# One attention chain over both token halves, two query tiles, two state tiles, and the recurrence's second half begun one attention step sooner

## The chip, the cores and the metric

The kernel runs on one core of a Trainium2 chip. A core has five engines that run side by side, each working through its own instructions strictly in the order in which they stand: TensorE (PE, matrix products; its weight loads are shown apart as PEld), VectorE (DVE), ScalarE (ACT), GpSimd (POOL) and SyncE (SP), which here issues nearly all DMAs. An instruction that waits for a semaphore holds up everything behind it on its engine; a DMA that waits on SP holds up the DMAs behind it.

The metric is the device time of the whole program in microseconds (us), lower is better, as the median of several runs. Of one execution there is also a profile; the times of instructions below come from that one.

## What is computed

One layer of a streaming encoder: a token mixer (sliding-window attention with sinks in one half of the channels, a gated linear recurrence in the other), a cross-attention into 256 memory tokens, and a SwiGLU feed-forward block, each between two RMSNorms. The change touches the token mixer alone. Its two halves, shortened:

```python
def swa_with_sinks(q, k, v, sinks):     # 8 query heads, 2 key heads, head size 64
    # a frame in chunk c (64 frames) reads every frame of chunks c-2 .. c
    s = einsum('bnqhgd,bnkhd->bhgqk', qc, kband) * 64 ** -0.5
    p = softmax(concat([s, sink]))[..., :L]
    return einsum(p, vband)

def hgrn2(q, f_logit, i, g, lb, onorm_g):    # 4 heads of 128
    # S_t = diag(f_t) S_{t-1} + k_t i_t^T,  o_t = S_t^T q_t, in chunks of 64
    ...
    return rms_norm(o, onorm_g) * silu(g)

u = rms_norm(x, g_mix_pre)
z = u @ w_in                        # 1024 -> 2816: q, k, v, and the recurrence's q, f, i, g
y = concat([ya, yh]) @ w_out
```

All tensors are float32; the token count is 2048 and the model width 1024. Products are made of three products of a high and a low part (a matmul on each pair but low times low).

## The kernel before

The 2048 tokens make 16 pairs of chunks of 128 tokens (NT = 16), and two halves of 1024 (NPB = 8 pairs each). `run` calls `mix`, which records the whole layer; a scheduler of the language then puts each engine's instructions in an order of its own, with dependencies kept, so that the order of recording is a priority and not the order on the chip.

`mix` goes through these stages:

- `in_first` makes the first half's input projection z and two blocks of 128 columns of the second half's. z goes to DRAM (`z_d`).
- The stage that the change touches runs three generators side by side, each cut into steps by `yield`: `swa` (attention, one pair of chunks a step), `hgrn` (recurrence, one pair a step) and `in_proj` (the second half's remaining 20 column blocks of the projection, 128 columns a step, long runs of matmuls of 128x512 in lines 156 to 158 that fill PE between the others' pieces). Before: first `swa` and `hgrn` over pairs 0 to 7 (lines 218 to 226), then a second `swa` over pairs 8 to 15 (lines 227 to 234) with the next column blocks and, in `side`, the sums of the output projection's weight blocks (`sums`, `combined`), which load `w_out` and store `out_s`.
- In the `xp` pool (lines 238 to 246) `fold_cross` folds the cross-attention's weights (32 steps), while `hgrn` runs over pairs 8 to 15 and `phases` prepares the output projection's tiles (splits written to `T`, loads `z<-in_w_out_dram`).
- After that `phases` makes the output projection, the cross-attention and the feed-forward block. That is the longest part, and the change does not touch it.

`swa` is a pipeline of two stages: at each step `swa_front` of one pair is recorded, then `swa_back` of the pair before. `swa_front` loads the queries of four heads (`qd`, lines 758 to 761), splits them on ACT (line 763) and DVE (line 764) into `qs`, does that again for the other four heads, loads the keys (`kr`, high part on POOL, low part on DVE, line 983 within `split2`), transposes the values (line 779), and makes scores (lines 798, 799), masked minimum (803) and exponential (807). `swa_back` transposes the probabilities (832), splits them (`pth` on ACT 836, `ptl` on DVE 837), multiplies by the values (841, 842) and stores. One call of `swa` takes one step more than it has pairs; the last step has only a back.

The tile `qd` has one buffer. The two query loads of a pair, and those of the next pair, therefore use the same memory one after the other. `qs` has two buffers.

`hgrn` is a pipeline of three stages: `hgrn_state` of pair n-1, `hgrn_front` of pair n, `hgrn_last` of n-2, `hgrn_out` of n-1. `hgrn_state` scales the state W of the pair before on POOL (line 907) and adds the new product on DVE (line 908) into a new tile W; `hgrn_out` multiplies the queries by the state that was there before (line 919). W has three buffers, each as large as a `qd` tile (512 floats a partition).

PSUM has eight banks here, of four kinds with two buffers each: g (the projection's), t, s and h. A generator is given the kinds that it may use: `swa` s and t in the first half, s, t and h in the second; `hgrn` h in the first, g and t in the second.

Of the kernel before, what the change touches and what calls it, by code (L numbers as in the profile page):

```python
# [11 lines left out]
F32 = mybir.dt.float32  # L12
# [6 lines left out]
P = 128  # L19
# [9 lines left out]
NPB = TB // P  # L29
NT = T // P  # L30
# [6 lines left out]
def f32(ap):  # L37
    return ap.bitcast(F32)
# [10 lines left out]
class Layer:  # L49
# [144 lines left out]
    def mix(self):  # L194
        tc, I = self.tc, self.I
        kw = dict(reuse_waits="tile")
        with contextlib.ExitStack() as left:
            def pool(name, at, **k):
                return at.enter_context(tc.tile_pool(name=name, bufs=1, **k, **kw))

            self.mc = pool("mc", left)
            self.r_x = self.cst.tile([P, NT], F32, name="r_x")
            with (
                tc.tile_pool(name="t1", bufs=3, **kw) as self.ts,
                tc.tile_pool(name="t2", bufs=3, **kw) as self.tb,
                tc.tile_pool(name="s1", bufs=2, side="right", **kw) as self.st_pool,
                contextlib.ExitStack() as at,
            ):
                self.banks(at, "ps1", **MOST)
                self.raws = 3  # L210
                u = self.in_first()
            self.banks(left, "ps2", **FOUR)
            self.hg = pool("hg", left)
            self.wp = pool("wp", left)
            self.io = pool("io", left)
            with tc.tile_pool(name="sw", bufs=1, side="right", **kw) as self.sw:
                self.zero_tiles()
                swa = self.swa(range(NPB), "st")
                hgrn = self.hgrn(range(NPB), "h")
                cols = self.in_proj(1, u)  # L220
                next(cols)
                for _ in swa:
                    next(hgrn)
                    next(cols)
                for _ in hgrn:
                    pass
                swa = self.swa(range(NPB, NT), "sth")
                self.out_sums, side = self.sums("out_s", self.w_out, 4, lambda: self.io_tile("u"), lambda: self.io_tile("x"))
                side = side()
                next(side)  # L230
                for _ in swa:
                    next(cols)
                    for _ in range(4):
                        next(side, None)
                for _ in cols:
                    pass
            phases = self.phases(self.jobs(), None, lambda: self.io_tile("z"))
            with tc.tile_pool(name="xp", bufs=1, side="right", **kw) as self.xp:
                fold = self.fold_cross()
                for i, _ in enumerate(self.hgrn(range(NPB, NT), "gt")):  # L240
                    for _ in range(2):
                        next(fold)
                    if 2 <= i < 10:
                        next(phases)
                for _ in fold:
                    pass
            left.close()
            with (
                tc.tile_pool(name="t3", bufs=3, **kw) as self.ts,
                tc.tile_pool(name="t4", bufs=3, **kw) as self.tb,  # L250
                tc.tile_pool(name="s3", bufs=2, side="right", **kw) as self.st_pool,
                contextlib.ExitStack() as at,
            ):
                self.banks(at, "ps3", **MOST)
                self.raws = 4
                for _ in phases:
                    pass
# [132 lines left out]
    def zero_tiles(self):  # L390
        nc, ph = self.nc, self.hg

        self.wmask = self.sw.tile([P, M], F32, name="wmask")
        nc.vector.memset(self.wmask, 0.0)
        nc.vector.memset(self.wmask[0:64, 192:256], BIG)
        nc.vector.memset(self.wmask[64:128, 0:64], BIG)

        cm = self.io.tile([P, P], F32, tag="u", name="cm", bufs=2)
        nc.vector.memset(cm, 1.0)
        nc.gpsimd.affine_select(cm, cm, [[1, P]], ALU.is_ge, 0.0, base=0, channel_multiplier=-1)  # L400
        nc.vector.memset(cm[0:64, 64:128], 0.0)
        self.cmask = ph.tile([P, P], I32, name="cmask")
        nc.vector.tensor_copy(self.cmask, cm)

        self.atz = []
        for i in range(2):
            a = ph.tile([P, 4, P], F32, name=f"atz{i}")
            nc.gpsimd.memset(a, 0.0)
            self.atz.append(a)
        self.vst_prev = None  # L410
        self.W = ph.tile([P, 4, P], F32, tag="W", name="W0", bufs=3)
        nc.gpsimd.memset(self.W, 0.0)

    ORDER = [(4, 5), (0, 1), (2, 3)] + [(10 + h, 6 + h) for h in range(4)] + [(c, c + 1) for c in range(14, 22, 2)]
# [334 lines left out]
    def swa_front(self, n, kinds):  # L749
        nc, ph = self.nc, self.sw  # L750
# [3 lines left out]
        kinds = itertools.cycle(kinds)  # L754

        qs = []
        for g in range(2):
            qd = ph.tile([P, 4, P], F32, tag="qd", name=f"qd{n}_{g}")
            qsrc = z[g * 256:(g + 1) * 256, t0:t0 + P].rearrange("(h d) t -> d h t", d=64)
            self.load(qd[0:64], qsrc)  # L760
            self.load(qd[64:128], qsrc)
            q = ph.tile([P, 4, P], F32R, tag="qs", name=f"qs{n}_{g}", bufs=2)
            nc.scalar.activation(q, qd, AF.Copy, scale=-0.125)
            nc.vector.scalar_tensor_tensor(q[64:128], qd[64:128], -0.125, f32(q[64:128]), ALU.mult, ALU.subtract)
            qs.append(q)
# [23 lines left out]
        for g in range(2):  # L789
            mn = self.small("w_mn", 4)  # L790
            den = self.small("w_den", 4)
            for i2 in range(2):
# [7 lines left out]
                for r in range(2):  # L800
                    i = 2 * i2 + r
# [98 lines left out]
    def hgrn_state(self, n, kinds, kt, vt):  # L900
        nc, ph = self.nc, self.hg
        prev = self.W
        W = self.W = ph.tile([P, 4, P], F32, tag="W", name=f"W{n}", bufs=3)
        ps = self.bank(kinds[0])
        for h in range(4):
            nc.tensor.matmul(ps[:, h * P:(h + 1) * P], kt[:, h, :], vt[:, h, :], start=True, stop=True)
        nc.gpsimd.tensor_tensor(W, prev, self.G[:, n, :, 1].unsqueeze(2).broadcast_to([P, 4, P]), ALU.mult)
        nc.vector.tensor_tensor(W, ps.rearrange("p (h t) -> p h t", h=4), W, ALU.add)
        return prev

    def hgrn_out(self, n, kinds, q6, at, vt, W):
        nc, ph = self.nc, self.hg
        sg = ph.tile([P, 4, P], F32, tag="sg", name=f"sg{n}")
        self.load(sg, self.z_d[C_GH:C_GH + 512, n * P:(n + 1) * P].rearrange("(h p) t -> p h t", p=P))
        ps = self.bank(kinds[-1])
        for h in range(4):
            hs = slice(h * P, (h + 1) * P)
            nc.tensor.matmul(ps[:, hs], at[:, h, :], vt[:, h, :], start=True, stop=False)
            nc.tensor.matmul(ps[:, hs], q6[:, h, :], W[:, h, :], start=False, stop=True)
        ss = self.small("h_ss", 4)  # L920
        on = ph.tile([P, 4, P], F32, tag="on", name=f"on{n}")
        for h in range(4):
            nc.scalar.activation(on[:, h, :], ps[:, h * P:(h + 1) * P], AF.Square, accum_out=ss[:, h:h + 1])
        vv = self.small("h_vv", 4)
        nc.gpsimd.tensor_scalar(vv, ss, 1.0 / P, EPS, ALU.mult, ALU.add)
        rs = self.small("h_rs", 4)
        nc.gpsimd.tensor_tensor(rs, vv, self.mhalf[:, 0:4], ALU.pow)
        nc.vector.tensor_tensor(on, ps.rearrange("p (h t) -> p h t", h=4),
                                rs.unsqueeze(2).broadcast_to([P, 4, P]), ALU.mult)
        return on, sg  # L930
# [28 lines left out]
    def swa(self, pairs, kinds):  # L959
        last = None  # L960
        for n in itertools.chain(pairs, (None,)):
            cur = None if n is None else (n, kinds) + self.swa_front(n, kinds)
            if last is not None:
                self.swa_back(*last)
            last = cur
            yield
# [783 lines left out]
```

## Time and profile before

| | |
|---|---|
| median of 3 runs | 2604.39 us (2603.98 to 2605.17) |
| profiled execution, its own time | 2610.75 us |
| its span, first to last instruction | 2609.0 us |
| mean granted TensorE clock | 0.996 |
| DMA moved | 506.03 MB, mean 194 GB/s |
| first attention instruction on `qs` to the last | 280.4 to 607.6 us |
| recurrence's last state update | 741.9 us |

The profiled execution is 6.36 us longer than the median of the runs shown; sums over its rows are differences, which are then taken off the median.

How to read what follows: a row of the page or of a view names the engine, the source line, what is written and read, the form and the count. "Idle before" is time in which that engine did nothing, with what ended it. In a table by stretches of time, the first column is the stretch in us from the span's start, then its length and, for each engine, busy time and number of instructions; then the granted TensorE clock (1.00 is full speed), the busy share of the DMA engines and GB/s.

### The profile page before, as it was taken

Reading aid. Unit: us, or ns where it says so; the run is one execution under the profiler, and the core shown is the slowest. Engines: PE = TensorE matmul, PEld = TensorE weight load, DVE = VectorE, ACT = ScalarE, POOL = GpSimd, SP = SyncE. Lnnn points to the kernel's source line nnn. Section 1 sums busy time; section 2 is a strip of 40 time slices with the busy share of each in tenths; the row PEclk is TensorE's granted clock in tenths of the full one; section 3 lists DMA queues with packets and bytes.
Section 4 is the critical chain, followed back from the end, with each engine's and each line's share of the span. In section 5 each row is a group of like instructions: output and inputs, shape, how many; then the busy total and the mean of one; then the engine's idle time right before and its main releaser. Section 6 shows DMA issues by size and latency. Waiting matters only on the chain.

```text
span 2609.0 us, 34953 instructions
## 1 busy us (share of the span) xinstructions
PE 2555.2 (98%) x12371; PEld 2138.3 (82%) x12371; DVE 1752.0 (67%) x2759; ACT 1259.7 (48%) x2633; POOL 435.2 (17%) x612
## 2 busy tenths in 40 slices
PE   9999999999999999999999999999999999999998
PEld 8878788787898887888878888888888888888886
DVE  7785488877555778778885655566666556564656
ACT  5553366555555556565563333344333334453543
POOL 4231334231311323222310000000000000000022
PEclk9999999999999999999999999999999999999999
DMA  5445655675887986765974622353566434576888
GB/s 186 145 162 177 172 160 157 192 228 157 239 269 268 308 288 231 222 233 186 317 248 131 202 93 75 105 194 121 177 200 196 154 130 159 191 210 177 264 215 219
DMA packets 363663, 506.03 MB, mean 194 GB/s; under 512 B 20960, under 2 KB 249312, under 8 KB 363488
## 3 DMA queue, kind: packets, MB, share of 16 engines
q1 hardware_dynamic: 357440, 481.77, 57.0%
q0 software_dynamic: 6048, 22.02, 4.7%
q8 instruction: 97, 1.59, 0.2%
q14 instruction: 78, 0.64, 0.1%
HBM read 337.00 MB, written 166.72 MB: 193 GB/s over the span
## 4 chain that ended last, share of the span: by engine, by line
PE 79%; DMA 9%; DVE 5%; ACT 3%; issue 2%; POOL 1%; SPq 0%; DVEq 0%; POOLq 0%; ACTq 0%
PE psm L1117 22%; PE psm L1119 22%; PE psm L1118 22%; PE psg L158 1%; PE psg L157 1%; PE psg L156 1%; PE pss L1369 1%; DMA qd<-z_d 1%; DMA z<-in_w_out_dram 1%; DMA row<-y_d 1%; ACT T L980 1%; DMA raw<-in_wo_x_dram 1%; DMA u_d<-row 1%; DVE T L983 0%; DMA row<-d_s 0%
## 5 line engine op out<-in xcount | busy, mean ns | idle before, releaser
L1117 PE MATMUL psm<-T,S 128*128 128x512 f32 x2695 | 1043.8, 391 | 12.1 <-ACT part L1132 9.3
L1118 PE MATMUL psm<-T,S 128*128 128x512 f32 x2695 | 1049.0, 390 | 2.1 <-DVE T L983 2.0
L1119 PE MATMUL psm<-T,S 128*128 128x512 f32 x2695 | 1038.5, 390 | 3.9 <-DVE S L983 3.9
L1117 PEld LDWEIGHTS psm<-T,S 128*128 128x128 f32 x2695 | 506.2, 188 | 121.7 <-ACT part L1132 9.6
L1119 PEld LDWEIGHTS psm<-T,S 128*128 128x128 f32 x2695 | 506.3, 188 | 110.7 <-DVE S L983 5.6
L1118 PEld LDWEIGHTS psm<-T,S 128*128 128x128 f32 x2695 | 506.3, 188 | 106.9 <-DVE T L983 3.7
L983 DVE TENSOR_TENSOR S<-sraw,S 128x512 fp32r<-128x512 f32 (+1 forms) x319 | 217.2, 688 | 215.4 <-ACT S L980 199.3
L980 ACT ACTIVATE S<-sum 128x512 fp32r<-128x512 f32 (+1 forms) x314 | 188.7, 619 | 358.1 <-PE psm L1119 269.3
L983 DVE TENSOR_TENSOR S<-sum,S 128x512 fp32r<-128x512 f32 (+1 forms) x372 | 249.7, 681 | 49.0 <-ACT S L980 32.9
L1132 ACT ACTIVATE part<-psm 128x512 f32<-128x512 f32 x273 | 161.7, 597 | 242.8 <-PE psm L1119 220.9
L980 ACT ACTIVATE S<-sraw 128x512 fp32r<-128x512 f32 (+1 forms) x272 | 167.4, 616 | 112.3 <-PE psm L1119 99.5
L1495 POOL DMA_DIRECT2D row<-y_d x28 | 25.8, 923 | 1112.7 <-DVE row L1681 1020.2
L983 DVE TENSOR_TENSOR T<-row,T 128x1024 fp32r<-128x1024 f32 (+1 forms) x120 | 141.5, 1194 | 58.2 <-ACT T L980 57.6
L156 PE MATMUL psg<-u,whi 128*128 128x512 f32 x320 | 129.5, 405 | 0.0
L1466 ACT ACTIVATE junk<-row 128x512 f32<-128x512 f32 x160 | 99.7, 624 | 60.9 <-DVE row L1488 29.5
L157 PE MATMUL psg<-u,whi 128*128 128x512 f32 x320 | 128.0, 400 | 0.0
L158 PE MATMUL psg<-u,wlo 128*128 128x512 f32 x320 | 127.9, 400 | 0.0
L980 ACT ACTIVATE T<-row 128x1024 fp32r<-128x1024 f32 x120 | 120.0, 1027 | 12.6 <-DMA row<-in_w_down_dram 5.2
L982 POOL TENSOR_SCALAR S<-sum 128x512 fp32r<-128x512 f32 x58 | 54.2, 935 | 292.9 <-PE psm L1119 231.4
L1632 DVE TENSOR_TENSOR row<-psm,part 128x512 f32<-128x512 f32 x66 | 43.7, 687 | 61.9 <-PE psm L1119 61.8
L1641 DVE TENSOR_TENSOR part<-psm,part 128x512 f32<-128x512 f32 x60 | 39.8, 688 | 62.4 <-PE psm L1119 62.2
L1092 DVE TENSOR_TENSOR sum<-sraw,sraw 128x512 f32<-128x512 f32 (+1 forms) x93 | 63.8, 686 | 18.9 <-DMA sraw<-in_w_in_dram 5.7
(362 smaller groups left out, 3695.6 us busy)
## 6 DMA issues: line engine op xcount, KB each, us to landing
sraw<-in_w_gate_dram SPq DMA_DIRECT2D x44, 512.0 KB, 3.9
sraw<-in_w_up_dram SPq DMA_DIRECT2D x44, 512.0 KB, 3.9
hid_d<-row SPq DMA_DIRECT2D x44, 512.0 KB, 2.7
h_d<-row SPq DMA_DIRECT2D x32, 512.0 KB, 5.1
y_d<-row SPq DMA_DIRECT2D x32, 512.0 KB, 3.5
sraw<-hid_d SPq DMA_DIRECT2D x32, 512.0 KB, 5.2
row<-y_d POOLq DMA_DIRECT2D x28, 512.0 KB, 7.3
sraw<-in_w_in_dram SPq DMA_DIRECT2D x44, 256.0 KB, 3.8
```

Source lines behind the costliest of these rows:

```text
L156: nc.tensor.matmul(ps, ah, bh, start=(i == 0), stop=False)
L157: nc.tensor.matmul(ps, ah, bl, start=False, stop=False)
L158: nc.tensor.matmul(ps, al, bh, start=False, stop=(i == n - 1))
L980: self.nc.scalar.activation(hi, raw, AF.Copy)
L982: self.nc.gpsimd.tensor_scalar(hi, raw, 1.0, 1.0, ALU.mult, ALU.mult)
L983: self.nc.vector.tensor_tensor(lo, raw, f32(hi), ALU.subtract)
L1092: nc.vector.tensor_tensor(t, a, b, op)
L1117: nc.tensor.matmul(ps, s[:, 0, k, :], t[:, 0, k, :], start=st, stop=False, **kw)
L1118: nc.tensor.matmul(ps, s[:, 0, k, :], t[:, 1, k, :], start=False, stop=False, **kw)
L1119: nc.tensor.matmul(ps, s[:, 1, k, :], t[:, 0, k, :], start=False, stop=sp, **kw)
L1132: nc.scalar.activation(t, ps, AF.Copy)
L1466: self.nc.scalar.activation(junk, a, AF.Square, scale=float(D) ** -0.5, accum_out=to)
```

## The change

The diff, whole but for its comments' place:

```diff
-                swa = self.swa(range(NPB), "st")
+                swa = self.swa(range(NT), lambda n: "st" if n < NPB else "sth")
                 hgrn = self.hgrn(range(NPB), "h")
                 cols = self.in_proj(1, u)
                 next(cols)
-                for _ in swa:
+                for _ in range(NPB + 1):
+                    next(swa)
                     next(hgrn)
                     next(cols)
                 for _ in hgrn:
                     pass
-                swa = self.swa(range(NPB, NT), "sth")
                 self.out_sums, side = self.sums("out_s", self.w_out, 4, ...)
                 side = side()
                 next(side)
-                for _ in swa:
+                pairs = self.hgrn(range(NPB, NT), "gt")
+                for i, _ in enumerate(swa, NPB + 2):
                     next(cols)
+                    if i == NT + 1 - 0:
+                        next(pairs)
                     for _ in range(4):
                         next(side, None)
                 for _ in cols:
                     pass
...
                 fold = self.fold_cross()
-                for i, _ in enumerate(self.hgrn(range(NPB, NT), "gt")):
+                for _ in range(2):
+                    next(fold)
+                for i, _ in enumerate(pairs, 1):
                     for _ in range(2):
                         next(fold)
                     if 2 <= i < 10:
                         next(phases)
...
-        self.W = ph.tile([P, 4, P], F32, tag="W", name="W0", bufs=3)
+        self.W = ph.tile([P, 4, P], F32, tag="W", name="W0", bufs=2)
...
-            qd = ph.tile([P, 4, P], F32, tag="qd", name=f"qd{n}_{g}")
+            qd = ph.tile([P, 4, P], F32, tag="qd", name=f"qd{n}_{g}", bufs=2)
...
-        W = self.W = ph.tile([P, 4, P], F32, tag="W", name=f"W{n}", bufs=3)
+        W = self.W = ph.tile([P, 4, P], F32, tag="W", name=f"W{n}", bufs=2)
...
     def swa(self, pairs, kinds):
         last = None
         for n in itertools.chain(pairs, (None,)):
-            cur = None if n is None else (n, kinds) + self.swa_front(n, kinds)
+            cur = None if n is None else (n, kinds(n)) + self.swa_front(n, kinds(n))
```

So there is one `swa` over all 16 pairs with 17 steps in place of two calls with 9 each: the front of pair 8 is recorded in the step with the back of pair 7, before the last step of the first recurrence and before the loads of `w_out`. The second half's loop has 8 steps and takes 8 column blocks and 32 pieces of `side` in place of 9 and 36; two column blocks in place of one remain after it. In its last step (i is 17, with the back of pair 15) the first step of the second recurrence is recorded, which is the front of pair 8. The first two steps of `fold_cross` come before the recurrence goes on; each later recurrence step stands beside the same fold steps as before, one recurrence step ahead. `qd` gets a second buffer and W loses its third.

## The prediction, made before the changed kernel was run

> **What bounds the kernel now.** I read the page first (busy time by engine, the chain that ended last), then the table by stretches over the part that the change touches, then what PE waited for there.
>
> ```profile
> span 2609.0 us, 34953 instructions
> PE 2555.2 (98%) x12371; PEld 2138.3 (82%) x12371; DVE 1752.0 (67%) x2759; ACT 1259.7 (48%) x2633; POOL 435.2 (17%) x612
> ...
> PE 79%; DMA 9%; DVE 5%; ACT 3%; issue 2%; POOL 1%; SPq 0%; DVEq 0%; POOLq 0%; ACTq 0%
> ```
>
> PE is the bound: 98% busy, 79% of the chain. The change adds and removes no matmul, so it can only shift PE's idle time, 2609.0 - 2555.2 = 53.8 us in all, and the time at half clock. The part that it touches is 283 to 790 us:
>
> ```profile
> core 0: us, PE busy (x) PEld busy (x) DVE busy (x) ACT busy (x) POOL busy (x), PEclk, DMA share, GB/s
> 283.00:310.00 27.00, 22.44 (x107) 19.04 (x108) 15.31 (x52) 10.93 (x42) 5.74 (x11) 0.87 0.69 182
> 310.00:500.00 190.00, 188.17 (x1102) 162.04 (x1101) 155.34 (x364) 120.11 (x351) 72.73 (x109) 1.00 0.53 157
> 500.00:520.00 20.00, 16.94 (x73) 13.04 (x72) 18.72 (x41) 11.29 (x33) 6.18 (x9) 0.91 0.99 260
> 520.00:640.00 120.00, 118.35 (x616) 99.11 (x615) 94.21 (x240) 66.79 (x185) 27.63 (x44) 1.00 0.60 186
> 640.00:660.00 20.00, 14.72 (x102) 12.62 (x102) 12.73 (x21) 12.52 (x29) 6.15 (x8) 1.00 0.96 271
> 660.00:690.00 30.00, 28.03 (x219) 27.35 (x219) 19.93 (x27) 14.72 (x31) 9.30 (x8) 0.94 0.85 237
> 690.00:790.00 100.00, 96.19 (x751) 91.80 (x750) 47.17 (x69) 52.32 (x129) 21.43 (x30) 1.00 0.81 262
> ```
>
> The steady stretches are full: 1.8 us idle in 310 to 500, 1.7 in 520 to 640. The idle time sits at four joints: the first attention steps (4.6 us), the change of halves at 500 (3.1), the change from attention to the fold at 640 (5.3) and the stretch after it (2.0). At three of them the granted clock also falls, which costs PE the stretch times what is missing from 1.00: 27 x 0.13 = 3.5 us, 20 x 0.09 = 1.8, 30 x 0.06 = 1.8. That makes joints of 8.1, 4.9, 5.3 and 3.8 us, 22.1 us in all. PE's waits in this part (us in total, times, longest) say what ended them:
>
> ```profile
> PE pst L798 <- DVE qs L764: 3.2, 1, 3.2
> PE psh L841 <- ACT pth L836: 3.0, 2, 2.8
> PE psg L890 <- ACT atz L881: 1.7, 1, 1.7
> PE pst L895 <- DMA v<-z_d: 1.5, 1, 1.5
> PE pss L798 <- DVE qs L764: 1.4, 1, 1.4
> ...
> PE pst L799 <- DVE kl L983: 0.9, 2, 0.6
> PE pst L879 <- ACT T L980: 0.8, 1, 0.8
> ...
> PE psg L906 <- ACT kt L892: 0.6, 1, 0.6
> ```
>
> **The change, part by part.** *Two query tiles.* With one tile, each query load waits until ACT and DVE have taken the one before. The chain of waits through the second pair's front shows it (start, length, what):
>
> ```profile
> 290.19 5.65 DMA qd<-z_d
> 295.95 0.64 ACT qs L763
> 296.61 1.11 DVE qs L764
> 297.74 0.58 SPq L75
> 298.37 3.13 DMA qd<-z_d
> 301.61 0.64 ACT qs L763
> 302.27 0.70 DVE qs L764
> 303.02 0.58 PE pst L798
> ```
>
> The second load is issued at 297.74, when DVE is done with the first, and PE waits for it until 303.02. With two tiles both loads leave together: in the changed program's order the second query load stands directly behind the first on SP, ahead of the keys, in this pair and the one before. The landing, SP's 0.58 and the second ACT and DVE pieces (3.13 + 0.64 + 0.70) then overlap the first's, and the 3.2 us wait with the clock loss behind it goes. What is new: the loads of keys and values stand behind two more query loads, and on DVE the second query piece stands ahead of the low key part, which PE waits for:
>
> ```profile
> L764 DVE SCALAR_TENSOR_TENSOR qs<-qd,qs x32: 689/690/1103, 281.1 to 607.6; 64x512 fp32r<-64x512 f32 x32
> ...
> DMA to landing us min/median/max: 2.7/3.5/8.2
> ```
>
> So of the 8.1 us I leave the key wait of 0.6 and one more DVE piece of 0.7, and take 8.1 - 1.3 = 6.8. Bounds: 8.1 if the keys land as before; 2.3 if the idle time only halves and the clock loss of 3.5 stays. The single wait of 1.4 (the fifth row of the waits) is the same tile at another pair: take 1.4, bounds 0 and 1.4.
>
> Here the Trainium skill ("TensorE: Matmul & The Clock Gate", section on the HAM clock gate) says that PE falls to half clock after a whole idle window of about 3.4 us. The rows above show the clock fall after single waits of 3.2 and 2.8, so the trace disagrees; by the rule none of these gaps would cost clock, and the first joint's term would be 6.8 - 3.5 = 3.3 us, an estimate.
>
> *One chain over both halves.* No drain and refill at pair 8. The joint at 500 is, though, a query wait too: ACT stood for a query load, and the probabilities' split that PE wanted (L836) stood behind it and its followers on ACT:
>
> ```profile
> 500.77 1.24 SPq L75 DMA_DIRECT2D qd<-z_d  x2
> ...
> 509.46 0.63 ACT L763 ACTIVATE qs<-qd 128x512 fp32r<-128x512 f32 x1 [4.06 <-DMA qd<-z_d]
> ...
> 512.05 0.57 ACT L836 ACTIVATE pth<-pss 128x512 fp32r<-128x512 f32 x1
> ```
>
> The load took 8 us, since it came behind a burst of `w_out` loads (DMA share 0.99). The second tile and a step of lead let it be issued before the burst: in the changed order pair 10's loads stand ahead of the larger part of it. But the burst stays, and another load may now be the late one (pair 9's keys stand behind two `w_out` loads). I take 3.0 of 4.9; bounds 0 and 4.9.
>
> *The recurrence one step sooner.* At 640 PE meets pair 8's front with nothing to cover it: waits of 1.7 (atz), 0.6 (kt) and 0.8 (pair 10's scores behind a `T` split on ACT). In the changed order pair 8's scores and value transposes stand among the matmuls of the last column block, and its key copy further ahead still, so those are covered: 3.1 us. The 1.5 for `v`, whose one buffer is free only after pair 8's transposes, I leave. Moved along are pair 8's four loads, which pass the remaining attention loads on SP, and 0.25 MB each (128 x 4 x 128 floats) is little beside the half megabyte of a column block's weights (128 x 8 x 128). Bounds 0 (the wait for `v` takes up what the others leave) and 5.3.
>
> In the stretch after it, ACT waited for a `w_out` load with the fold's weight split behind it:
>
> ```profile
> 672.74 1.06 ACT L980 ACTIVATE T<-z 128x1024 fp32r<-128x1024 f32 x1 [6.53 <-DMA z<-in_w_out_dram]
> 673.71 1.04 ACT L980 ACTIVATE whi<-raw 128x1024 fp32r<-128x1024 f32 x1
> ```
>
> In the changed order this weight split and the next stand ahead of that `T` split, so PE has two more column blocks to work on before the DMA matters. I take 2.0 of 3.8; bounds 0 and 3.8.
>
> *Two state tiles.* The scaling of the state (POOL) now overwrites the tile that the output of the pair before still reads (L919), so it must wait for those matmuls; behind it on POOL stand the query scaling, the norm's small pieces, key splits and the weight splits of the projection.
>
> ```profile
> L907 POOL TENSOR_TENSOR W<-W,G x16: 1042/1044/2022, 261.7 to 731.9; 128x512 f32<-128x512 f32 x16
> ...
> L908 DVE TENSOR_TENSOR W<-psg,W x8: 680/682/693, 649.2 to 741.9; 128x512 f32<-128x512 f32 x8
> ...
> 726.91 0.39 PE L919 MATMUL pst<-W,q 128*128 128x128 f32 x2
> ...
> 729.17 0.69 DVE L908 TENSOR_TENSOR W<-psg,W 128x512 f32<-128x512 f32 x1 [3.98 <-PE psg L906]
> ```
>
> One of the tighter places: output read at 726.91, next state add at 729.17, so 2.3 us of room for a scaling of 1.04. That fits, with PE working on the fold meanwhile. If it stops fitting, each pair costs at most 1.04 + 0.68 = 1.7 us, 15 pairs 25.9. I take 1.0; bounds 0 and 25.9.
>
> *Another order everywhere in the stage.* The scheduler reorders some thousand PE rows. The next row that could move is the 1.8 us of the long steady stretch (a gain at best); at worst there is another joint like that at 500, 4.9 us. I take a loss of 2.5.
>
> **Sum.** 6.8 + 1.4 + 3.0 + 3.1 + 2.0 - 1.0 - 2.5 = 12.8 us. The profiled execution took 2610.75 us by its own clock (span 2609.0 and 1.75 around it), so the like of it would be 2598.0. It lies 6.36 above the median of the runs, and 2604.4 - 12.8 = 2591.6 us.
>
> **The rivals.**
> 1. *The joints from 500 on are bound by DMA, not by the order.* For it: DMA shares of 0.99, 0.96, 0.85 there, and a query load that took 8 us. Against it: the shares fall to 0.60 between, so work can be shifted, and the waits named are ACT's order. Then only the two query terms remain: 6.8 + 1.4 - 1.0 - 2.5 = 4.7, 2599.7 us.
> 2. *The change does not do what it says.* The waits that leave are replaced by waits for keys or values that land as late, since attention loads were late by the burst and by landing times of 2.7 to 8.2 us, whatever their buffer. Against it: the 5.7 us from one query landing of the pair to the other (290.19 + 5.65 to 298.37 + 3.13) are plain. 2604 us, give or take 3.
> 3. *Slower: the two state tiles.* POOL waits for PE's output matmuls at each pair, and PE then waits for the splits behind. For it: POOL runs in order, and the room is only 2.3 us late in the fold. Against it: the page has POOL busy for 17% of the span, and the table by stretches for 73 of the 190 us of the long steady one. Full price: 13.8 of gains without W, less 25.9, is 12.1 us slower, 2616.5 us. It decides from 13.8 / 15 = 0.9 us a pair on.
>
> **How the numbers follow.** Chances: forecast 0.62, first rival 0.17, second 0.09, third 0.12. A measurement of this kernel can tell about 0.2%, 5.2 us, from no change. Faster than 2599.2: 0.61 of the forecast and 0.08 of the first rival, 0.69. Within: 0.01, 0.09 and 0.06, 0.16. Slower than 2609.6: 0.12 and 0.03, 0.15. All upper bounds together (23.5 us) give 2580.9, which is unlikely; the range of 2583 to 2607 leaves some 0.05 below and 0.14 above, and the forecast's own range is 2584 to 2599.
>
> **What would show it.** Right: in the first attention steps no PE wait of over 1.5 us for `qs` and a clock of 1.00 after 300 us; query loads issued in pairs of two halves each; ACT's waits for `qd` well below before; pair 8's front inside the last column block; no PE wait for atz at the fold's start. Wrong: POOL waiting at L907 (L912 in the changed file) for PE with kh or whi late behind it; PE waits for kh or kl that grow by what the query waits lose; a new half-clock stretch in 430 to 640. Everything from 790 us on should be as before but earlier; a difference there would mean that something I did not price has moved.

## The result, and the profile after

The changed kernel took 2592.02 us (median of 6 runs, 2587.06 to 2595.59) against 2604.65 for the kernel before: a ratio of 0.9948, 95% interval 0.9937 to 0.9960, 12.6 us faster. The forecast was 2591.6.

The page of the changed kernel's profiled execution (2587.36 us), the lines that answer to those of before:

```profile
span 2585.7 us, 34998 instructions
...
PE 2548.3 (99%) x12371; PEld 2135.9 (83%) x12371; DVE 1747.9 (68%) x2759; ACT 1261.0 (49%) x2633; POOL 428.4 (17%) x612
...
PE 83%; DMA 7%; DVE 4%; ACT 3%; issue 2%; POOL 1%; SPq 0%; DVEq 0%; POOLq 0%; ACTq 0%
```

PE's idle time in the span fell from 53.8 to 37.4 us (2585.7 - 2548.3), and its busy time, for the same matmuls, by 6.9 us, in part because PE ran less at half clock (mean granted clock 0.998, before 0.996). The same stretches as before:

```profile
283.00:310.00 27.00, 27.00 (x151) 23.22 (x150) 19.01 (x66) 15.63 (x54) 6.26 (x14) 1.00 0.76 216
310.00:500.00 190.00, 189.43 (x1104) 163.94 (x1103) 159.78 (x367) 124.40 (x361) 75.21 (x115) 1.00 0.58 176
500.00:520.00 20.00, 19.57 (x102) 16.18 (x102) 19.70 (x52) 10.77 (x31) 5.34 (x7) 1.00 1.08 324
...
640.00:660.00 20.00, 20.00 (x168) 19.83 (x168) 14.30 (x18) 11.85 (x26) 3.80 (x6) 1.00 0.94 254
660.00:690.00 30.00, 28.80 (x243) 28.57 (x242) 13.96 (x24) 14.53 (x41) 12.79 (x16) 1.00 0.76 248
```

The first steps lose nothing now (before: 4.6 us idle and clock 0.87). The change from attention to the fold has moved forward, to 620 to 640 us, as all in front of it takes less time:

```profile
620.00:640.00 20.00, 16.62 (x105) 14.95 (x104) 10.94 (x16) 11.44 (x25) 3.20 (x5) 0.91 0.89 246
```

Here 3.4 us are idle and 20 x 0.09 = 1.8 lost to the clock. That is one of the prediction's signs of being wrong, a new half-clock stretch in 430 to 640 us; in the second execution of the changed kernel (below) this stretch lost 3.2 us and no clock. PE's longest waits from 270 to 790 us, in all, times and longest:

```profile
PE pst L900 <- DMA v<-z_d: 1.7, 1, 1.7
PE pst L900 <- ACT whi L126: 1.2, 1, 1.2
PE psg L895 <- issue: 1.2, 1, 1.2
PE psh L158 <- DVE wlo L988: 1.0, 1, 1.0
```

No wait for `qs` is left, and the first row is the wait for `v` that the prediction left in place. What the two new tile counts did shows in the views of the tiles. First what the instructions on `qd` waited for, and the landing times (the first row is that of before):

```profile
  DMA qd<-z_d: 56.7, 18
...
  ACT qs L768: 9.4, 5
  DMA qd<-z_d: 3.7, 2
...
DMA to landing us min/median/max: 2.7/3.3/6.2
```

ACT stood for query loads 56.7 us in 18 waits before, and 3.7 us in two now. Then the view of line 912, the scaling of the state on POOL (907 before), with what it waited for, and who waited for it:

```profile
L912 POOL TENSOR_TENSOR W<-W,G x16: 1042/1046/2005, 259.4 to 716.6; 128x512 f32<-128x512 f32 x16
...
  PE pst L924: 25.7, 4
  PE psh L924: 10.1, 3
...
who waited for it (us, times):
  DVE W L913: 1.7, 1
```

POOL does stand for the output's matmuls, 35.8 us in seven waits, but only one state addition waits for the scaling itself, 1.7 us, and no wait of PE in this part names POOL.

The two first profiles differ by 23.4 us, the medians by 12.6: the first execution of before was a long one, that of the changed kernel a short one. So every term below is read from medians, and from the profiles only where, and by what wait.

### The profile page after: what moved, and what is told of

It reads as the page before. It is cut to its first block, busy times and chain, and to the rows that moved or that the text cites. A ratio compares the mean times of both kernels' runs of the same rounds, so it can differ in the third digit from the quotient of the medians.

```text
span 2585.7 us, 34998 instructions
## 1 busy us (share of the span) xinstructions
PE 2548.3 (99%) x12371; PEld 2135.9 (83%) x12371; DVE 1747.9 (68%) x2759; ACT 1261.0 (49%) x2633; POOL 428.4 (17%) x612
## 4 chain that ended last, share of the span: by engine, by line
PE 83%; DMA 7%; DVE 4%; ACT 3%; issue 2%; POOL 1%; SPq 0%; DVEq 0%; POOLq 0%; ACTq 0%
PE psm L1122 23%; PE psm L1124 23%; PE psm L1123 22%; PE psg L156 2%; PE psg L157 2%; PE psg L158 2%; PE pss L1374 1%; DMA row<-y_d 1%; DMA raw<-in_wo_x_dram 1%; DMA u_d<-row 1%; DMA h1t_d<-row 1%; DMA row<-h_d 1%; ACT junk L1471 1%; ACT T L985 0%; PE pss L837 0%
## 5 line engine op out<-in xcount | busy, mean ns | idle before, releaser
L812 ACT ACTIVATE S<-S,w_mn 128x256 f32<-128x256 f32 (+1 forms) x128 | 63.1, 495 | 28.6 <-DVE w_mn L808 28.3
```

Source lines behind the costliest of these rows:

```text
L812: nc.scalar.activation(s[:, r, o:], s[:, r, o:], AF.Exp, bias=mn[:, i:i + 1], scale=-1.0, accum_out=den[:, i:i + 1])
```

## The experiments

All runs, with the kernel before run on the same chip beside them:

| kernel | query tiles | state tiles | one chain | early recurrence | median us (range) | before | ratio (95%) |
|---|---|---|---|---|---|---|---|
| before, again | 1 | 3 | no | no | 2603.8 (2601.1 to 2611.7) | 2604.7 | 1.0002 (0.9991 to 1.0012) |
| changed, again | 2 | 2 | yes | yes | 2591.9 (2588.0 to 2596.1) | 2604.7 | 0.9955 (0.9942 to 0.9968) |
| state tiles alone | 1 | 2 | no | no | 2604.3 (2598.2 to 2609.1) | 2604.7 | 0.9997 (0.9988 to 1.0006) |
| query tiles | 2 | 2 | no | no | 2609.8 (2604.8 to 2615.9) | 2604.7 | 1.0021 (1.0011 to 1.0032) |
| chain alone | 1 | 3 | yes | no | 2610.3 (2606.8 to 2612.8) | 2604.9 | 1.0016 (1.0005 to 1.0026) |
| chain, state tiles | 1 | 2 | yes | no | 2602.6 (2598.5 to 2609.6) | 2604.0 | 0.9988 (0.9978 to 0.9998) |
| early alone | 1 | 3 | no | yes | 2604.1 (2600.0 to 2608.9) | 2604.9 | 0.9999 (0.9990 to 1.0008) |
| changed, one query tile | 1 | 2 | yes | yes | 2598.8 (2597.3 to 2612.5) | 2604.9 | 0.9983 (0.9972 to 0.9994) |
| changed, late recurrence | 2 | 2 | yes | no | 2598.0 (2595.8 to 2603.2) | 2604.9 | 0.9975 (0.9965 to 0.9984) |
| changed, two calls | 2 | 2 | no | yes | 2603.4 (2598.6 to 2607.2) | 2604.1 | 0.9996 (0.9987 to 1.0004) |
| query tiles, blocks held | 2 | 2 | no | no | 2600.1 (2596.4 to 2609.8) | 2604.1 | 0.9984 (0.9973 to 0.9995) |
| changed, still sooner | 2 | 2 | yes | sooner | 2592.7 (2586.3 to 2599.6) | 2604.1 | 0.9955 (0.9941 to 0.9969) |

**Both kernels again.** No edit.

> The kernel before, unchanged: a second profiled execution of it, since the first one (2610.75 us) lay 6 us above the median of the runs (2604.4). If the idle time of the four joints belongs to the program, PE again has some 15 us idle in 283 to 690 us and three stretches at half clock, at the first attention steps, near 513 and near 677 us. If the half-clock stretches are a matter of the single execution, the shorter execution (2602 to 2606) lacks one or two of them, 2 to 4 us each, and the median gain of the change is smaller than the difference of the two first profiles (23.4 us) for that reason.

> The changed kernel, unchanged: a second profiled execution, since the first one (2587.36 us) was the shortest but one of six (median 2592.0). Expected 2592 us, plus or minus 2. If the joints' gain belongs to the program, the first attention steps again run without a wait for qs and at clock 1.00, and what the longer executions have more lies elsewhere. If the gain at the first steps is luck, a half-clock stretch shows there again, 3.4 us.

The second execution of before (2606.71 us), three of its stretches:

```profile
283.00:310.00 27.00, 22.88 (x119) 19.68 (x118) 15.56 (x51) 10.93 (x42) 5.67 (x12) 0.94 0.66 183
...
500.00:520.00 20.00, 19.55 (x102) 16.18 (x101) 17.22 (x40) 10.38 (x28) 4.71 (x7) 1.00 0.98 264
...
640.00:660.00 20.00, 16.27 (x112) 15.03 (x113) 12.17 (x18) 11.23 (x27) 10.06 (x11) 0.91 1.01 282
```

The first steps and the joint at 640 belong to the program: 4.1 and 3.7 us idle with a half-clock stretch each. The joint at 500 does not. It lost 4.9 us in the first execution and 0.45 in this one. The changed kernel's second execution has the first stretch full and at clock 1.00 again. At 500 it is now the changed kernel that loses, 2.2 us, after 0.4 in its first execution:

```profile
500.00:520.00 20.00, 17.78 (x90) 14.24 (x89) 17.29 (x46) 9.08 (x28) 6.09 (x7) 1.00 1.08 287
```

**Two query tiles, two state tiles; two state tiles alone.** In the kernel before:

```diff
-        ... tag="W", name="W0", bufs=3)
+        ... tag="W", name="W0", bufs=2)
-        ... tag="W", name=f"W{n}", bufs=3)
+        ... tag="W", name=f"W{n}", bufs=2)
```

and, for the run with two query tiles, also

```diff
-            qd = ph.tile([P, 4, P], F32, tag="qd", name=f"qd{n}_{g}")
+            qd = ph.tile([P, 4, P], F32, tag="qd", name=f"qd{n}_{g}", bufs=2)
```

> The kernel before with two query tiles and, to make room for the second, two state tiles; two attention calls and the recurrence's start as before. By my sum: 6.8 us at the first steps and 1.4 at the single wait, less 1.0 for the state tiles, so about 7 us faster, 2597 (2594 to 2601). If the two later edits carry the change and keys land as late as queries did, less than 3 us faster, 2602 or more. If the query tile carries everything, 12 us faster, 2592.

> The kernel before with two state tiles in place of three and nothing else. By my sum 1 us slower, 2605.5 (2604 to 2607). By the rival that POOL's wait for the output matmuls stops the splits behind it, up to 1.7 us a pair, 10 to 25 us slower, 2614 or more. If the scaling is hidden everywhere, no difference.

The state tiles cost nothing. The query tiles, in place of gaining 7 us, lost 5. The run with two query tiles, stretches of its profile:

```profile
283.00:310.00 27.00, 27.00 (x149) 23.06 (x148) 19.04 (x68) 15.37 (x53) 6.11 (x13) 1.00 0.78 220
...
620.00:640.00 20.00, 14.99 (x71) 10.44 (x70) 17.36 (x40) 13.14 (x31) 1.59 (x5) 0.91 0.52 160
640.00:660.00 20.00, 13.86 (x75) 12.60 (x76) 12.14 (x17) 13.07 (x29) 6.02 (x7) 0.74 0.98 253
```

The first steps gain as forecast, and it is given back at the next joint: from 620 to 640, 5.0 us idle and 1.8 of clock, from 640 to 660, 6.1 and 5.2. PE's timeline there shows the waits (in brackets), and the row below it is ACT's:

```profile
621.20 0.39 PE L158 MATMUL psg<-u,wlo 128*128 128x512 f32 x1
...
629.39 0.50 PE L841 MATMUL psh<-pth,vst 128*128 128x512 f32 x1 [2.24 <-ACT pth L836]
...
643.26 2.07 PE L906 MATMUL psg<-vt,kt 128*128 128x128 f32 x8 [4.83 <-ACT vt L897]
```

```profile
641.51 1.06 ACT L980 ACTIVATE T<-z 128x1024 fp32r<-128x1024 f32 x1 [6.27 <-DMA z<-in_w_out_dram]
```

The longest of these waits is not attention's: PE stands 4.8 us for the recurrence's `vt`, which ACT makes, and ACT had stood 6.3 us for a load of `w_out`. Attention's part lies before it. The projection's last matmul is at 621.2. All the matmuls of attention's last steps that stand behind it have nothing to cover their waits for ACT and DVE, as PE's groups from 621.3 to 640 us show (shapes, count, busy, mean, idle before):

```profile
L842 PE MATMUL psh<-ptl,vst 128*128 128x512 f32 x8 | 4.4, 555 | 0.0
L841 PE MATMUL psh<-pth,vst 128*128 128x512 f32 x8 | 4.0, 494 | 3.2 <-ACT pth L836 3.2
L832 PE MATMUL pss<-ident,S 128*128 128x128 f32 x12 | 3.4, 334 | 0.0
L832 PE MATMUL pst<-ident,S 128*128 128x128 f32 x12 | 3.3, 327 | 0.2 <-DVE w_mn L803 0.2
```

That is 24 transposes and 16 products. In the first profile of before they are no transpose and 4 products, in the changed kernel none: there the last product starts at 623.89 and the projection's last matmul at 624.79. The projection gets ahead of attention with two query tiles, and it was the cover (that is, the work that keeps PE busy while attention's pieces wait).

**One chain alone; early recurrence alone.**

```diff
-                swa = self.swa(range(NPB), "st")
+                swa = self.swa(range(NT), lambda n: "st" if n < NPB else "sth")
...
-                for _ in swa:
+                for _ in range(NPB + 1):
+                    next(swa)
                     next(hgrn)
                     next(cols)
...
-                swa = self.swa(range(NPB, NT), "sth")
```

> The kernel before with one attention chain over both halves, and nothing else: one query tile, three state tiles, the recurrence's second half begun in the fold as before. By my sum 3.0 us faster, 2601.7 (2599 to 2605): the joint near 500 us mends, the first steps and the joint near 640 stay. New theory, from the run with two query tiles: what decides at 640 is how much of attention's tail (lines 832, 841, 842) is left when the projection's matmuls end; there it was 24 transposes and 16 products, with two state tiles alone 8 and 12. The chain starts attention's second half a step sooner, so by it no such matmul is left behind the projection's end and the joint near 640 mends as well: 5 to 8 us faster, 2597 to 2600.

```diff
-                for _ in swa:
+                pairs = self.hgrn(range(NPB, NT), "gt")
+                for i, _ in enumerate(swa, NPB + 1):
                     next(cols)
+                    if i == NT + 1:
+                        next(pairs)
...
-                for i, _ in enumerate(self.hgrn(range(NPB, NT), "gt")):
+                for _ in range(2):
+                    next(fold)
+                for i, _ in enumerate(pairs, 1):
```

> The kernel before with the recurrence's second half begun in the last step of the second attention call, and nothing else. By my sum 3.1 at 640 us and 2.0 behind it, 5 us faster, 2599.6 (2597 to 2603). By the new theory attention's tail sets that joint, and pair 8's front ahead of it pushes the tail further behind the projection's end: less than 2 us faster, or slower, 2603 to 2608.

Neither gains. The chain alone is 5 us slower, though no product of attention stands behind the projection's end in it; so the tail is not all there is. Two places in its profile, PE's timeline and ACT's waits from 520 to 600 us:

```profile
549.81 0.79 PE L842 MATMUL psh<-ptl,vst 128*128 128x512 f32 x1 [2.89 <-DVE ptl L837]
...
645.09 1.62 PE L879 MATMUL pst<-qq,k 128*128 128x192 f32 x4 [5.28 <-DMA k<-z_d]
```

```profile
ACT qs L763 <- DMA qd<-z_d: 13.3, 4, 6.6
```

With one query tile a query load fell into the burst of `w_out` loads (DMA share 1.07 from 540 to 550 us, landing up to 11.5 us in this run), ACT stood for it 6.6 us, and PE went on at half clock behind the 2.9. (DVE, whose `ptl` PE waited for, had itself stood 4.1 us for the DMA `out_s<-u` until 545.88, so the query load is one of two late DMAs there.) At 640 the next pair's scores wait 5.3 us for keys of the recurrence. The early recurrence alone moved a wait: pair 8's front is covered, and PE stands for the next pair's query load:

```profile
652.83 0.89 PE L884 MATMUL pst<-qq,k 128*128 128x192 f32 x4 [3.16 <-DMA qq<-z_d]
```

**The chain with two state tiles.** As the chain alone, with W's two edits from above.

> One attention chain with one query tile, as in the run that was 5 us slower, but with two state tiles as in the changed kernel, so that the three edits can be set against each other with the state tiles alike. If the chain with one query tile is slower because a query load falls into the burst of w_out loads (there PE lost 2.9 us and its clock near 550 us) and because pair 8's loads are late at 640, it is slower again, 2607 to 2612, with ACT waiting for qd by 5 us or more in 520 to 600. If that loss was a chance of one order of the scheduler, which other state tiles shift, it is as before or faster, 2600 to 2605.

2602.6 us, 7.7 less than with three state tiles (6.8 less when each is taken from the runs of before beside it). In its profile ACT's waits for `qd` from 520 to 600 us are

```profile
ACT qs L763 <- DMA qd<-z_d: 3.6, 4, 1.5
```

So the second expectation came true: the loss of the chain alone was of one order, which other tile counts shift. How the scheduler comes to that order was not followed.

**The changed kernel, one part undone at a time.** One query tile (`bufs=2` taken away from `qd`):

> The changed kernel with one query tile, all else as changed (one chain, two state tiles, early recurrence). By my sum it loses 8.2 us against the changed kernel: 2600 (2597 to 2602), with the wait for qs and the half-clock stretch back at the first attention steps. By the rival that the order carries the change and the second query tile brings nothing in the end, as it brought nothing alone: 2592 to 2595.

The recurrence begun in the fold as before:

```diff
-                pairs = self.hgrn(range(NPB, NT), "gt")
-                for i, _ in enumerate(swa, NPB + 2):
+                for _ in swa:
                     next(cols)
-                    if i == NT + 1 - 0:
-                        next(pairs)
...
-                for _ in range(2):
-                    next(fold)
-                for i, _ in enumerate(pairs, 1):
+                for i, _ in enumerate(self.hgrn(range(NPB, NT), "gt")):
```

> The changed kernel with the recurrence's second half begun in the fold as before, all else as changed (one chain, two query tiles, two state tiles). By my sum it loses 5 us against the changed kernel: 2597 (2595 to 2600). By the new theory the chain has put attention's tail under the projection already, and pair 8's front alone is left uncovered at 640: 3 to 5 us lost, and no matmul of attention behind the projection's end. If the early start is what mends the joint that two query tiles spoiled, it loses 10 us or more, 2602 or higher.

Two attention calls (the two query and state tiles of the earlier run, with the early recurrence's edit):

> The changed kernel without the single chain: two attention calls, two query tiles, two state tiles, the recurrence's second half begun in the second call's last step. In PE's order 24 transposes and 16 products of attention stand behind the projection's end, as with two query tiles alone. By the theory of the tail the chain is what takes them away, and this kernel is not faster than before: 2604 to 2610. By my sum it loses only the 3.0 us of the chain against the changed kernel: 2595.

Against the changed kernel's 2591.9 the three lose 6.9, 6.1 and 11.5 us. With one query tile the wait is back, in the first steps' stretch and in PE's waits:

```profile
283.00:310.00 27.00, 23.55 (x121) 19.97 (x120) 17.16 (x62) 12.92 (x47) 6.12 (x12) 0.94 0.59 165
```

```profile
PE pst L803 <- DVE qs L769: 2.7, 1, 2.7
```

That is 3.5 us idle and 1.6 of clock, 5.1 of the 6.9. With the late recurrence the two waits of pair 8's front are back that were named for before:

```profile
PE psg L890 <- ACT atz L881: 2.1, 1, 2.1
PE psg L906 <- ACT kt L892: 1.3, 1, 1.3
```

With two calls attention's tail lies behind the projection again, and the joint costs 4.9 us idle and 3.8 of clock:

```profile
620.00:640.00 20.00, 15.10 (x72) 12.15 (x71) 14.37 (x26) 11.86 (x22) 0.20 (x1) 0.81 0.66 195
```

The changed kernel lost 3.4 and 1.8 in that stretch (above), so 3.5 of the 11.5 us are seen here. From 620 to 690 us, idle time and clock together, this kernel loses 10.8 us, and the changed kernel 6.4 and 5.5 in its two executions. In attention's tail there PE waits 2.9 us for `ptl`, 2.1 of it at once. The execution that was profiled is the shortest of 11, 4.9 us under their median.

**Query tiles, column blocks held back.** As the run with two query tiles, and

```diff
-                for _ in swa:
-                    next(cols)
+                for i, _ in enumerate(swa):
+                    if i > 2:
+                        next(cols)
```

> Two query tiles and two state tiles in the kernel before, as in the run that was 5 us slower, but the second attention call's first three steps take no column block of the projection, so that four are left at its end. In the order of PE's instructions 8 transposes and 12 products of attention then stand behind the projection's end, as with two state tiles alone, in place of 24 and 16. By the theory of attention's tail the joint near 640 us costs about what it costs with two state tiles alone, and the gain at the first steps stays: 2598 to 2601. If the two query tiles lose elsewhere, or the tail is not what costs, it stays at 2607 to 2611.

2600.1, within the expected 2598 to 2601: with 20 matmuls of attention behind the projection in place of 40 the kernel is 9.7 us faster. Its one profile (2609.79 us) is of the longest of 12 executions, but the joint can be read in it:

```profile
620.00:640.00 20.00, 16.06 (x91) 12.89 (x89) 15.22 (x31) 13.33 (x28) 1.01 (x3) 1.00 0.63 190
640.00:660.00 20.00, 17.05 (x110) 16.02 (x109) 14.49 (x20) 12.79 (x29) 6.79 (x9) 0.83 1.13 264
```

That is 6.9 us idle and 3.4 of clock, 10.3 in all, where the run without the hold lost 18.1 and two state tiles alone, also with 20 behind, 10.6. So the joint gave back 7.8 of the 9.7 us. It does not part the tail from the late load: ACT's longest wait for a load of `w_out` in 625 to 700 us fell with it, from 6.3 to 2.6 us.

**The recurrence sooner still.** `if i == NT:` in place of `NT + 1 - 0`.

> The changed kernel with the recurrence's second half begun one attention step sooner still, with the back of pair 14. What is left at the joint is PE's wait for v (1.7 us) and a half-clock stretch near 633 us. If the loads of pair 8 are what is late there, an earlier start takes 2 to 4 us more: 2588 to 2590. If it collides with attention's own tail, or v's one buffer decides, no gain or a loss: 2592 to 2597.

2592.7: no gain. In its profile the 1.7 us wait for `v` is gone from PE's list, and in its place

```profile
PE pst L900 <- DVE on L933: 3.4, 1, 3.4
PE psg L884 <- ACT mT L126: 1.8, 1, 1.8
PE pst L923 <- ACT vt L902: 1.6, 1, 1.6
```

## Why the prediction was right, and where it was not

The time came out at 0.4 us from the forecast, in a sum with two wrong terms.

*Two query tiles* (6.8 + 1.4 = 8.2): right in company, with the wait and the place that were named; undoing them in the changed kernel costs 6.9 us. The 8.1 us from which the term was taken were one execution's: the second lost 4.1 idle and 1.6 of clock there. The clock did not fall after the wait of 3.2 us, as the prediction reads it, but in its midst, at 301.51 us.

*The recurrence one step sooner* (3.1 + 2.0 = 5.1): right in size, 6.1 when undone, but only the 3.1 shows where it was placed, in the waits for `atz` and `kt` (2.1 + 1.3). The 2.0 for the stretch from 660 to 690 us does not: with the late recurrence that stretch lost 0.3 us, and in the changed kernel's two executions 1.2 and 1.8. That the size fits is in part luck. The wait for `v` stayed, as said.

*Two state tiles* (1.0): 0.4 us faster by the medians, and the interval holds no loss over 0.06%, 1.6 us. The third rival, slower through POOL, is out: POOL waits, and of PE's waits only one of 0.3 us, in the second execution, is for the state's addition behind it.

*One chain over both halves* (3.0): mis-sized. Undone it costs 11.5 us. The term was read from a joint at 500 us that lost 4.9 us in one execution and 0.45 in the next, and with the change 0.4 and 2.2, so no run shows that the chain mends it. What the chain is seen to bring beside two query tiles lies elsewhere: it keeps attention's last steps among the projection's matmuls. The prediction's part on the chain spoke of "no drain and refill at pair 8", never of where the last pair's drain falls.

*Another order everywhere* (2.5 loss, at worst 4.9): the step that failed. The orders of single edits cost more than their gains. From the kernel with two state tiles on (2604.3), two query tiles cost 5.5 us where the sum had a gain of 8.2, some 14 us off; the chain's time changes by 7.7 with the number of state tiles. The edits' effects do not add: alone they come to 5.5 (query tiles), -1.7 (chain) and, taken from its own run beside before, -0.8 (early recurrence), 3 us slower in sum (each known to some 3 us), while together they are 12.4 faster. Undone one at a time they are worth 6.9 + 11.5 + 6.1 = 24.5, twice the whole. The sum of 12.8 lay between these by luck as much as by reading: a chain term that was too small stood for an interaction that it did not know.

The first rival (the joints from 500 us on are bound by DMA, 4.7 us gained) is out for the whole, since undoing the chain or the early start loses 11.5 or 6.1 us; in single edits it was right: there PE or ACT stood for a late load next (`qq` 3.2, `k` 5.3, `z` 6.3 on ACT). The second (keys take the place of queries) is out: of waits for attention's keys PE has none in the changed kernel's first execution and 0.2 us in the second.

That the joint at 640 is a matter of the tail's cover rests on the run with held blocks, which hit its expected time and lost 7.8 us less at the joint, and on the two runs with 40 matmuls behind it, each slower than its counterpart with fewer (2609.8 against 2600.1, 2603.4 against 2591.9). It is not the whole rule: two state tiles alone leave 20 behind and lose nothing in time, the chain alone leaves none and is slower, and a `w_out` load that comes late at the joint is a rival that no run parts from it. Of the chain's 11.5 us some 5 are seen at the joint; where the rest comes from stays open: executions of one kernel differ by some 10 us, and one profile of each does not resolve 8 us spread over 300.

## What to carry to other kernels

Where a scheduler orders the engines, price an edit by the order that it makes, in the built program, and not by the wait that it removes: count which matmuls still stand behind the end of the work that covers them, as a first question and not as a rule. Test a change of several parts by undoing one part at a time as well as by adding one, since a part that loses alone (a second buffer, here 5 us) can be worth 7 in company. Read a joint's cost from two executions before giving it a term.

## What the runs showed of the hardware

The loss at half clock comes in pieces. In the records of the granted clock up to 2560 us, each stretch at a half is 3.41 us long, or two or three times that, and costs PE 1.7 us a piece. Within one execution the stretches begin on a grid of 3.413 us: in the first profile of before at 301.51, 513.13, 676.97 and 1328.92 us, which lie 62, 48 and 191 times 3.413 apart. What PE idles between two points of this grid decides. In the chain alone, around PE's wait of 2.89 us that ends at 549.81:

```profile
546.27:549.68 3.41, 0.65 (x3) 0.19 (x2) 3.38 (x4) 1.71 (x3) 2.94 (x2) 1.00 1.05 346
549.68:553.09 3.41, 3.28 (x11) 2.98 (x12) 3.35 (x13) 1.92 (x7) 0.00 (x0) 0.50 0.89 327
```

In the early recurrence alone, around the wait of 3.16 us that ends at 652.83, on the grid of its own stretch at 302.79 us:

```profile
647.53:650.95 3.42, 2.13 (x20) 1.90 (x18) 2.09 (x4) 2.17 (x9) 2.04 (x2) 1.00 1.02 338
650.95:654.36 3.41, 1.53 (x12) 1.56 (x13) 1.45 (x4) 2.97 (x10) 0.73 (x2) 1.00 1.08 339
654.36:657.77 3.41, 3.41 (x30) 3.41 (x29) 3.41 (x6) 1.27 (x2) 2.84 (x3) 1.00 1.16 283
```

The shorter wait lay in one window of the grid, 2.8 us idle, and the next window ran at a half. The longer one was shared by two windows, 1.3 and 1.9 us idle, and cost no clock. In all 14 profiles every one of the 45 full-clock windows with 1.93 us idle or more was followed by half clock, 16 of the 59 with 1.44 to 1.93, and none with less. The border may be sharper than that, since the ends of PE's matmuls are modelled. The grid lies otherwise in each execution (a point at 301.51 us in the first of before, at 303.08 in the second, 1.57 apart), so the same wait can cost clock in one and not in another.

The Trainium skill ("TensorE: Matmul & The Clock Gate", "Part 1: The HAM clock gate") has a free-running window of about 3.4 us: the grid agrees with it. That the window must be idle as a whole does not agree: 2.8 us were enough here.
